# Six scaled pairs in the convolved feed-forward, and fewer resident constants in a two-block kernel

## The chip, the cores and the metric

The kernel runs on one core of a Trainium2 chip. The metric is the device time of one execution in microseconds (us). Before the change it is 1011.3 us, the median of three runs (1009.15 to 1011.61).

Names of the engines: PE is TensorE, which multiplies matrices; DVE is VectorE; ACT is ScalarE; POOL is GpSimd; SP is SyncE, which here only issues transfers. SBUF is the memory that all engines work from, 128 partitions wide; PSUM holds the results of matmuls, in banks of 512 float32 columns.

## The reference, cut to what matters

One sequence of 256 tokens, width 1024, float32, passes two blocks.

```
# first block
hn = rms_norm(h, norm_mix_pre);  p = hn @ w_in            # 6912 columns
p_rw, p_ret, g_rw, g_ret = split(p)
y_rw  = rwkv7_mixer(p_rw, ...)      # 8 heads of 64, state S_t = S diag(w) + rank-one terms, over 256 steps
y_ret = retention_mixer(p_ret, positions)  # 8 heads, rotary q and k (64), v (128), decay masks, silu(g) * norm(o)
merged = sigmoid(g_rw) * (y_rw @ w_branch_rw) + sigmoid(g_ret) * (y_ret @ w_branch_ret)
h = h + rms_norm(merged @ w_out, norm_mix_post)
u = rms_norm(h, norm_ffn_pre) @ ffn_w_up                  # 2 x 2816 columns
u = causal depthwise convolution of width 3 over tokens + bias
gate, val = split(u)
h = h + rms_norm((gelu(gate) * val) @ ffn_w_down, norm_ffn_post)
# second block: SwiGLU, then spatial gating and Mamba-2 side by side, SwiGLU, a gated injection, a final norm
```

The second block isn't touched by the change, but it takes its buffers from the same slab.

## The kernel before, in words

**Weights.** All weights are read once, as a stream of 335 chunks of 128 x 1024 float32 values, eight 128 x 128 tiles each, in the order of use. A chunk is loaded by SP into one of six stage buffers. ACT copies it to float16 (hi) and DVE writes the rest, stage minus hi, as bfloat16 (lo); there are nine hi and lo buffers. A product is three matmuls (hi x hi, hi x lo, lo x hi), so a tile of 128 output columns from 1024 inputs is 24 matmuls of 256 token columns (`mtile`). `token_major` makes products with tokens on the partitions, by matmuls of 512 columns.

**Slab.** Everything that is neither stream, constants nor the residual h lies in one slab of SBUF, SLAB = 32,688 float32 columns. `Slab.get` hands out columns in the order of the program, `Buf.free` gives them back. A buffer that is laid over room used before has to wait until the last user of that room is done. `get` prefers a gap whose last user is planned to end before the new buffer is first needed (hints from the round of planning before), and among these it packs.

**Order of work.** The program is first recorded as a list of operations with their dependences. `Plan.run` is a list planner with a price for each operation and a due time from a run backwards; `Plan.issue` then emits every engine's instructions in the planned order. There are four rounds, each with the slab laid out anew from the times of the one before, and the best plan of the last three is taken. On the chip each engine runs its list in order and waits on semaphores, SP too: a transfer that waits holds up the stage loads behind it.

**First block.** `BlockOne.run` streams w_in: six tiles on the unscaled input, then scaled ones; the value part of retention (RET_V), rotated q and k, the retention gate (RET_G), then 16 tiles of branch gates. Beside these, two generators are stepped by `tick`: `rwkv` and `retention`. They use four "side" PSUM banks, the stream four "main" ones. RET_G fills all four main banks, two at a time; `evac_g` empties each: a tanh on ACT into a new 512-column buffer, then a DVE operation in place. Only after that can the next gate tile have the bank.

`rwkv` prepares four pairs of heads (from w2a2, a selector sel8t, and the RWKV columns), builds the score matrices m4, then solves 32 x 32 triangular systems: lt holds the factors, x starts as a constant (eye32), and 31 steps of two DVE operations each work on x and tmp. x and tmp are written to DRAM (scr_g, scr_h) and read back in other layouts into gb, hb and rb, which POOL has set to zero. Then two chunks of 128 tokens follow one after the other, a norm, and the product with g2.

`retention` works on two quads of heads. For each it multiplies scores by a decay table (3072 columns for both, loaded once) and by the values (2048 columns, both quads together).

**Feed-forward.** `post_norm` ends w_out and also yields xs, the input of the feed-forward without the norm's scaling by row. `up_pairs` makes 22 pairs of a gate and a value tile, each pair in one bank of 512 columns; seven main banks are there in this stage. Pairs 0 to 3 multiply xs, and `evac` scales their results by the norm (a DVE operation of 512 columns out of PSUM), so that PE needn't wait for the norm. Pairs from 4 on multiply `later`, the input scaled by `normed`, and need no scaling. In `evac` follow, for each half of the pair, an ACT operation and two DVE operations of the convolution, then gelu, the product and the split of the result.

Of the kernel before, what the change touches and what calls it, by code (L numbers as in the profile page):

```python
# [45 lines left out]
ZONE = 14000  # L46
ROUNDS = 4
FIRST = 4.0
SLAB = 32688
DECAY_C = float(np.exp(-0.5))  # L50
# [572 lines left out]
class Program:  # L623
# [260 lines left out]
    def up_pairs(self, gname, gbase, uname, ubase, xs, evac, later=None, chunked=False):  # L884


        banks = [self.pair() for _ in range(4)]
        self.mtiles_outer([b[:, 0:T] for b in banks], gname, [("c", gbase + i * P) for i in range(4)], xs, chunked)
        for i in range(NFF):
            if i < 4:  # L890
                bank = banks[i]
            else:
                xs = later or xs
                bank = self.pair()
                self.mtile(bank[:, 0:T], gname, range(NK), ("c", gbase + i * P), xs)
            self.mtile(bank[:, T : 2 * T], uname, range(NK), ("c", ubase + i * P), xs)
            self.done(lambda i=i, bank=bank: evac(i, bank))
        self.flush()
# [97 lines left out]
class BlockOne:  # L996
# [64 lines left out]
    def rwkv(self):  # L1061
        pr = self.pr
        V, S, PE, mm = pr.V, pr.S, pr.PE, pr.PE.matmul
        k_ = pr.k
        w2a2, g2 = pr.col("w2a2", 0, 512), pr.col("g2", 0, 512)
        self.AR, self.B, self.K, self.F = [], [], [], []
# [35 lines left out]
        for t in range(4):  # L1102
# [30 lines left out]
            bank = pr.bank()  # L1133
            mm(bank[:, 0:T], lhsT=k_["sel8t"][:, t * P : t * P + P], rhs=rk.ap, start=True, stop=True)
            kk = pr.buf(T)
# [81 lines left out]
            yield  # L1217
        rk.free()
        self.wdad.free()


        gb, hb, rb = pr.buf(1024), pr.buf(2048), pr.buf(512)
        for b in (gb, rb, hb):
            pr.G.memset(b.ap, 0.0)

# [23 lines left out]
        tv = tmp.v("p (i c) -> p i c", i=32)  # L1249
        V.tensor_copy(x.ap, k_["eye32"])  # L1250
        for j in range(31):
# [5 lines left out]
            if j % 4 == 3:  # L1257
                yield
        V.tensor_copy(tmp.v("p (c i) -> p i c", c=16), xv)
        sg = pr.dram("scr_g", (2, 4, 16, 32, 16))  # L1260
        sh = pr.dram("scr_h", (2, 4, 16, 16, 32))
        pr.plan.sync.dma_start(out=sg.rearrange("a b h i c -> (a b h) (i c)"), in_=x.ap)
        pr.plan.sync.dma_start(out=sh.rearrange("a b h c i -> (a b h) (c i)"), in_=tmp.ap)
        hcs = lambda b: b.v("p (h n) -> p h n", h=16)
        gv, hv, rv = hcs(gb), hcs(hb), hcs(rb)
        for b in range(4):
            s = slice(32 * b, 32 * b + 32)
            for half in range(2):
# [5 lines left out]
                pr.plan.sync.dma_start(out=d, in_=sh[half, b].rearrange("h c i -> c h i"))  # L1274
        for b in (lt, x, tmp):
            b.free()
# [97 lines left out]
        for b in (u, ut, b2, state, hb, m4, r0, vt, bt, kt0, *self.AR, *self.F):  # L1374
            b.free()
        rs = pr.buf(16)
        pr.rsqrt_small(rs.ap, stat.v("p (n k) -> p n k", k=2)[:, :, 1], 16, 1.0, 64e-5)
# [9 lines left out]
        for t in range(4):  # L1387
            bank = pr.bank()
            for c in range(2):
                pr.transpose(bank[:, c * P : c * P + P], ytv[:, c, t * P : t * P + P])  # L1390
            mm(bank[:, T : 2 * T], lhsT=g2[:, t * P : t * P + P], rhs=self.gd.ap, start=True, stop=True)
            o = pr.buf(T)
            S.activation(o.ap, bank[:, 0:T], AF.Identity, scale=pr.col("rw_lnx_w", t), bias=pr.col("rw_lnx_b", t))
            V.tensor_tensor(out=o.ap, in0=o.ap, in1=self.bv[t].ap, op=ADD)
            V.tensor_tensor(out=o.ap, in0=bank[:, T : 2 * T], in1=o.ap, op=MUL)
            self.bv[t].free()
            pr.unbank(bank)
            self.y_rw.append(pr.split(o.ap))
            o.free()
            yield  # L1400
        yt.free()
        self.gd.free()

# [24 lines left out]
    def retention(self):  # L1428
# [3 lines left out]
        for quad in range(2):  # L1432
# [4 lines left out]
            ov = oq[quad].v("p (c n) -> p c n", c=2)  # L1437
            qs, kk = self.rot["q", quad], self.rot["k", quad]
            for pair in range(2):
                banks = [pr.bank(), pr.bank()]  # L1440
# [5 lines left out]
                for i, bank in enumerate(banks):  # L1446
                    h = 4 * quad + 2 * pair + i
                    s = pr.buf(384)
                    V.tensor_tensor(out=s.ap, in0=bank[:, 0 : 3 * P], in1=pr.k["decay"][:, 3 * P * h : 3 * P * h + 3 * P], op=MUL)
                    pr.unbank(bank)  # L1450
                    ss.append(s)
# [3 lines left out]
                for i, s in enumerate(ss):  # L1455
                    h = 4 * quad + 2 * pair + i
                    e = slice(P * i, P * i + P)
                    v0, v1 = self.vr[:, 0, h * P : h * P + P], self.vr[:, 1, h * P : h * P + P]
                    mm(pov[:, 0, e], lhsT=s[:, 0:P], rhs=v0, start=True, stop=True)
                    mm(pov[:, 1, e], lhsT=s[:, P : 2 * P], rhs=v0, start=True, stop=False)  # L1460
                    mm(pov[:, 1, e], lhsT=s[:, 2 * P : 3 * P], rhs=v1, start=False, stop=True)
                    s.free()
                S.activation(ov[:, :, 2 * pair * P : 2 * (pair + 1) * P], pov, AF.Copy)
                pr.unbank(po)
                yield
            for b in qs + kk:
                b.free()
            yield
            for c in range(2):
# [7 lines left out]
                yield  # L1477
        self.vrb.free()
        ov = lambda c, h, n=1: oq[h // 4][:, c * 512 + (h % 4) * P : c * 512 + (h % 4) * P + n * P]
# [33 lines left out]
    def evac_v(self, c, nh, ps):  # L1513
        self.pr.S.activation(self.vr[:, c, 512 * nh : 512 * nh + 512], ps, AF.Copy)

# [14 lines left out]
    def run(self):  # L1530
# [35 lines left out]
        for j, (what, i, c) in enumerate(order):  # L1566
# [11 lines left out]
            if j == 8:  # L1578
                self.angles(pr.ins["pos"])
        dec = pr.buf(3072)  # L1580
        pr.plan.sync.dma_start(out=dec.ap, in_=pr.ins["decay"])
        pr.k["decay"] = dec.ap
        self.vrb = pr.buf(2048)
        self.vr = self.vrb.v("p (c n) -> p c n", c=2)
        pr.token_major("w_in", RET_V, xs, self.evac_v)
# [19 lines left out]
        pr.finish(g_ret)  # L1605
        dec.free()

# [33 lines left out]
        def evac(i, bank):  # L1641
            src, p = bank, None
            if i < 4:
                p = pr.buf(2 * T)
                V.tensor_tensor(out=p.v("p (g n) -> p g n", g=2), in0=bank.rearrange("p (g n) -> p g n", g=2),
                                in1=n2.rb.ap.unsqueeze(1).to_broadcast([P, 2, T]), op=MUL)
                src = p.ap
# [432 lines left out]

_KEEP = ("ones", "ident", "sel2", "sel8t", "inv", "mask", "blk64", "eye32")


def build(tc, ins, out, at, at2):
    nc = tc.nc
    with tc.tile_pool(name="sb", bufs=1) as sb, \
# [6 lines left out]
        hall = sb.tile([P, NK * T], F32, name="h")  # L2093
        cst = sb.tile([P, ins["cst"].shape[1]], F32, name="cst")
        kt = sb.tile([P, sum(ins[n].shape[1] for n in _KEEP)], F32, name="konst")
# [17 lines left out]
def program(pr, hall, kt):  # L2113
# [20 lines left out]
    load("ones", "ident")  # L2134
    load("sel2", "sel8t", "inv")
    pr.plan.sync.dma_start(out=pr.cst[:, nv:], in_=ins["cst"][:, nv:])
    pr.ws.load_to(3)
    load("mask", "blk64", "eye32")
    pr.power = pr.buf(16)
# [35 lines left out]
```

## Time and profile before

| | |
|---|---|
| median of three runs | 1011.3 us (1009.15 to 1011.61) |
| profiled execution | 1015.67 us |
| its span, first to last instruction | 1013.9 us |
| busy: PE, DVE, ACT, POOL | 983.4, 794.5, 613.8, 34.6 us |
| mean granted clock of PE | 0.988 of full speed |
| read from HBM | 185.35 MB, 185 GB/s over the span |

The profile is of one execution. A row of a timeline gives the start and the length of an operation, its engine, the line that issued it (here nearly always L484, the loop in `issue`), what it writes and reads, its form, and in brackets how long the engine stood idle before it and what ended that wait. Matmuls are pipelined, so their lengths overlap; the distance between starts is what one costs. The granted clock has two levels, 2.4 GHz (1.00) and 1.2 GHz (0.5); a stretch in between is a mix.

### The profile page before, as it was taken

What the parts mean: (1) busy time and instruction counts of PE and PEld (TensorE: products, weight loads), DVE (VectorE), ACT (ScalarE), POOL (GpSimd) and SP (SyncE); (2) the same over time, 40 slices, a digit from 0 to 9 for tenths busy, and PEclk for the clock granted to TensorE, in tenths of its full rate; (3) what the DMA queues carried; (4) which work ended last, traced back from release to release, by engine and by line L of the source; (5) the groups of instructions that cost most, each with busy time, mean ns of one, the idle gap of its engine ahead of it and who ended that gap; (6) DMA issues with size and microseconds to landing.
All of it is one profiled execution on the core that took longest, in us unless ns stands there. A gap on an engine that the chain in (4) does not pass through costs nothing.

```text
span 1013.9 us, 22086 instructions
## 1 busy us (share of the span) xinstructions
PE 983.4 (97%) x8884; PEld 830.6 (82%) x8899; DVE 794.5 (78%) x1515; ACT 613.8 (61%) x1042; POOL 34.6 (3%) x35
## 2 busy tenths in 40 slices
PE   8999996999998999999999999999999999999996
PEld 6766745998987888889888888768887888888884
DVE  7999698679888999756977756589798987776654
ACT  6774432545686877556655545577899665554543
POOL 2100000100001000000000000000000000000000
PEclk9899998999999999999999999999999999999999
DMA  9646656246636766664766666655545686666621
GB/s 344 233 150 197 183 166 194 74 155 224 204 96 220 218 203 204 204 197 140 236 204 204 200 198 205 198 179 161 198 124 173 201 273 205 202 196 205 198 75 42
DMA packets 60790, 189.68 MB, mean 187 GB/s; under 512 B 13184, under 2 KB 14992, under 8 KB 60176
## 3 DMA queue, kind: packets, MB, share of 16 engines
q1 hardware_dynamic: 59824, 185.39, 58.6%
q10 hardware_dynamic: 864, 2.89, 0.8%
q8 instruction: 69, 1.13, 0.5%
q14 instruction: 33, 0.27, 0.1%
HBM read 185.35 MB, written 1.85 MB: 185 GB/s over the span
## 4 chain that ended last, share of the span: by engine, by line
PE 71%; DVE 15%; ACT 6%; DMA 4%; issue 3%; POOL 1%; SPq 0%; POOLq 0%; ACTq 0%; DVEq 0%
PE main L484 44%; PE side L484 27%; DVE slab L484 11%; DVE lo L484 4%; ACT slab L484 3%; ACT hi L484 1%; DMA stage<-stream 1%; DMA slab<-scr_cs 1%; PE side L237 1%; DVE h L484 1%; POOL slab L484 1%; ACT L484 1%; DMA slab<-scr_l 1%; DMA h<-xt 1%; DMA scr_cs<-slab 0%
## 5 line engine op out<-in xcount | busy, mean ns | idle before, releaser
L484 PE MATMUL main<-slab,hi 128*128 128x256 f16 (+2 forms) x3276 | 553.7, 270 | 11.9 <-DVE slab L484 10.3
L484 PEld LDWEIGHTS <-hi 128*128 128x128 f16 x5080 | 489.3, 99 | 73.4 <-issue 13.3
L484 ACT ACTIVATE hi<-stage 128x1024 f16<-128x1024 f32 (+1 forms) x338 | 351.8, 1047 | 277.2 <-PE main L484 172.1
L484 DVE TENSOR_TENSOR lo<-stage,hi 128x1024 bf16<-128x1024 f32 (+1 forms) x338 | 406.8, 1210 | 139.3 <-ACT hi L484 138.5
L484 PE MATMUL main<-slab,lo 128*128 128x256 f16 (+1 forms) x1638 | 438.5, 272 | 0.4 <-DVE lo L484 0.4
L484 PE MATMUL side<-slab,hi 128*128 128x256 f16 (+3 forms) x1804 | 278.4, 260 | 2.0 <-DVE slab L484 1.1
L484 PEld LDWEIGHTS <-lo 128*128 128x128 bf16 x2540 | 249.2, 98 | 33.2 <-issue 3.7
L484 PE MATMUL side<-slab,lo 128*128 128x256 f16 (+1 forms) x902 | 225.3, 262 | 0.0
L484 DVE TENSOR_TENSOR slab<-slab 128x256 f32<-128x256 f32 (+13 forms) x427 | 165.5, 405 | 18.0 <-ACT slab L484 15.6
L484 ACT ACTIVATE slab<-slab 128x256 f32<-128x256 f32 (+4 forms) x302 | 116.7, 419 | 34.1 <-DVE slab L484 25.1
L484 PE MATMUL main<-hi,slab 128*128 128x512 f16 (+3 forms) x304 | 83.4, 357 | 0.6
L484 PEld LDWEIGHTS <-slab 128*128 128x128 f16 (+1 forms) x521 | 47.8, 101 | 42.6 <-issue 3.0
L484 ACT ACTIVATE slab<-side 128x128 f32<-128x128 f32 (+5 forms) x93 | 32.1, 379 | 51.8 <-PE side L484 42.5
L484 PEld LDWEIGHTS side<-slab 128*128 128x128 f32 x376 | 51.8, 192 | 8.4 <-DVE slab L484 4.4
L484 PE MATMUL side<-slab 128*128 128x64 f32 (+3 forms) x379 | 56.1, 264 | 2.5 <-DVE slab L484 2.3
L484 POOL TENSOR_TENSOR slab<-slab 128x2 f32<-128x2 f32 (+2 forms) x19 | 28.9, 1518 | 838.5 <-DVE slab L484 825.7
L484 PE MATMUL main<-lo,slab 128*128 128x512 bf16 (+3 forms) x138 | 48.5, 354 | 0.0
L484 DVE TENSOR_TENSOR slab<-side,slab 128x512 f32<-128x512 f32 (+4 forms) x58 | 32.7, 579 | 11.0 <-PE side L484 5.4
L484 DVE SCALAR_TENSOR_TENSOR slab<-main,cst,slab 128x255 f32<-128x255 f32 (+2 forms) x88 | 38.8, 469 | 1.6 <-ACT slab L484 1.5
L484 DVE SCALAR_TENSOR_TENSOR slab<-h,cst,slab 128x256 bf16<-128x256 f32 (+2 forms) x88 | 35.4, 427 | 2.3 <-ACT slab L484 2.2
L484 ACT ACTIVATE slab<-main 128x256 f32<-128x256 f32 (+2 forms) x66 | 25.3, 402 | 15.3 <-DMA scr_g<-slab 6.9
L484 DVE TENSOR_TENSOR slab<-main,slab 128x256 f32<-128x256 f32 (+1 forms) x53 | 28.6, 550 | 5.7 <-PE main L484 4.2
(60 smaller groups left out, 400.9 us busy)
## 6 DMA issues: line engine op xcount, KB each, us to landing
stage<-stream SPq DMA_DIRECT2D x332, 512.0 KB, 4.3
slab<-scr_cs SPq DMA_DIRECT2D x1, 2048.0 KB, 9.3
stage<-stream SPq DMA_DIRECT2D x6, 256.0 KB, 5.5
slab<-decay SPq DMA_DIRECT2D x1, 1536.0 KB, 8.4
slab<-slab SPq DMA_DIRECT2D x32, 32.0 KB, 1.9
slab<-last ACTq DMA_DIRECT2D x1, 1024.0 KB, 7.0
slab<-cst ACTq DMA_DIRECT2D x1, 1024.0 KB, 11.2
h<-xt SPq DMA_DIRECT2D x3, 256.0 KB, 6.1
```

What stands on the lines that cost most here:

```text
L237: op = self.new("PE", lambda: [fn(*args, **kw) for _, fn, args, kw in calls], (), {})
L484: o.fn(*o.args, **o.kw)
```

## The change

- The slab grows by 2048 columns, to 34,736. The room comes from constants that are no longer resident: w2a2 and g2 (1024 columns of cst), sel8t and eye32 (1024 of the constants).
- `rwkv` loads w2a2 and sel8t into slab buffers at its start and frees them after the four pairs of heads. x is loaded from eye32 by a transfer, where DVE copied it. lt is freed after the solve, and gb, hb and rb are taken and zeroed after it, where they were taken before it. g2 is loaded near the end.
- `retention` loads the decay table in two halves, one for each quad, and the values lie in two buffers of 1024; table and values are freed after their quad.
- RAW = 6: pairs 0 to 5 of the convolved feed-forward multiply xs and are scaled at eviction; `later` is used from pair 6 on.

```diff
-SLAB = 32688
+RAW = 6
+SLAB = 34736
@@ up_pairs
         for i in range(NFF):
+            if i >= RAW:
+                xs = later or xs
             if i < 4:
                 bank = banks[i]
             else:
-                xs = later or xs
                 bank = self.pair()
@@ rwkv
-        w2a2, g2 = pr.col("w2a2", 0, 512), pr.col("g2", 0, 512)
+        w2a2b, selb = pr.buf(512), pr.buf(512)
+        a = pr.at["w2a2"][0]
+        pr.plan.sync.dma_start(out=w2a2b.ap, in_=pr.ins["cst"][:, a : a + 512])
+        pr.plan.sync.dma_start(out=selb.ap, in_=pr.ins["sel8t"])
+        w2a2 = w2a2b.ap
...
-            mm(bank[:, 0:T], lhsT=k_["sel8t"][:, t * P : t * P + P], rhs=rk.ap, start=True, stop=True)
+            mm(bank[:, 0:T], lhsT=selb[:, t * P : t * P + P], rhs=rk.ap, start=True, stop=True)
...
-        rk.free()
+        for b in (rk, selb, w2a2b):
+            b.free()
         self.wdad.free()
-        gb, hb, rb = pr.buf(1024), pr.buf(2048), pr.buf(512)
-        for b in (gb, rb, hb):
-            pr.G.memset(b.ap, 0.0)
...
-        V.tensor_copy(x.ap, k_["eye32"])
+        pr.plan.sync.dma_start(out=x.ap, in_=pr.ins["eye32"])
...
         V.tensor_copy(tmp.v("p (c i) -> p i c", c=16), xv)
+        lt.free()
...
         pr.plan.sync.dma_start(out=sh.rearrange("a b h c i -> (a b h) (c i)"), in_=tmp.ap)
+        gb, hb, rb = pr.buf(1024), pr.buf(2048), pr.buf(512)
+        for b in (gb, rb, hb):
+            pr.G.memset(b.ap, 0.0)
...
-        for b in (lt, x, tmp):
+        for b in (x, tmp):
             b.free()
...
+        g2b = pr.buf(512)
+        a = pr.at["g2"][0]
+        pr.plan.sync.dma_start(out=g2b.ap, in_=pr.ins["cst"][:, a : a + 512])
...
-            mm(bank[:, T : 2 * T], lhsT=g2[:, t * P : t * P + P], rhs=self.gd.ap, start=True, stop=True)
+            mm(bank[:, T : 2 * T], lhsT=g2b[:, t * P : t * P + P], rhs=self.gd.ap, start=True, stop=True)
@@ retention
+            dec = pr.buf(1536)
+            pr.plan.sync.dma_start(out=dec.ap, in_=pr.ins["decay"][:, 1536 * quad : 1536 * quad + 1536])
...
-                    V.tensor_tensor(out=s.ap, in0=bank[:, 0 : 3 * P], in1=pr.k["decay"][:, 3 * P * h : 3 * P * h + 3 * P], op=MUL)
+                    d = 3 * P * (h % 4)
+                    V.tensor_tensor(out=s.ap, in0=bank[:, 0 : 3 * P], in1=dec[:, d : d + 3 * P], op=MUL)
...
-            for b in qs + kk:
+            for b in (*qs, *kk, dec, self.vrb[quad]):
                 b.free()
@@ run
-        dec = pr.buf(3072)
-        pr.plan.sync.dma_start(out=dec.ap, in_=pr.ins["decay"])
-        pr.k["decay"] = dec.ap
-        self.vrb = pr.buf(2048)
-        self.vr = self.vrb.v("p (c n) -> p c n", c=2)
+        self.vrb = [pr.buf(1024) for _ in range(2)]
+        self.vr = [b.v("p (c n) -> p c n", c=2) for b in self.vrb]
...
-            if i < 4:
+            if i < RAW:
                 p = pr.buf(2 * T)
@@ build, program
-_KEEP = ("ones", "ident", "sel2", "sel8t", "inv", "mask", "blk64", "eye32")
+_KEEP = ("ones", "ident", "sel2", "inv", "mask", "blk64")
...
-        cst = sb.tile([P, ins["cst"].shape[1]], F32, name="cst")
+        cst = sb.tile([P, at["end"][0]], F32, name="cst")
...
-    load("sel2", "sel8t", "inv")
-    pr.plan.sync.dma_start(out=pr.cst[:, nv:], in_=ins["cst"][:, nv:])
+    load("sel2", "inv")
     pr.ws.load_to(3)
-    load("mask", "blk64", "eye32")
+    load("mask", "blk64")
```

## Rows read from the trace of the kernel before

**Rows 1.** The page's first line and first part: busy us, share of span, instructions.
```profile
span 1013.9 us, 22086 instructions
PE 983.4 (97%) x8884; PEld 830.6 (82%) x8899; DVE 794.5 (78%) x1515; ACT 613.8 (61%) x1042; POOL 34.6 (3%) x35
```

**Rows 2.** Waits of PE: us in total, times, longest.
```profile
PE main L484 <- DVE slab L484: 11.5, 4, 9.0
```

**Rows 3.** Table by stretch: length, busy us (instructions), clock, DMA share, GB/s.
```profile
30.00:40.00 10.00, 9.47 (x62) 7.58 (x61) 8.04 (x19) 7.61 (x15) 2.95 (x1) 0.66 0.59 201
...
176.00:181.00 5.00, 4.94 (x26) 3.49 (x25) 0.60 (x1) 1.44 (x4) 0.00 (x0) 0.53 0.48 64
...
317.00:322.00 5.00, 5.00 (x33) 3.83 (x31) 5.00 (x13) 2.32 (x5) 0.00 (x0) 0.66 0.09 36
330.00:390.00 60.00, 60.00 (x551) 53.09 (x549) 59.90 (x114) 46.36 (x80) 0.00 (x0) 1.00 0.70 210
420.00:460.00 40.00, 40.00 (x405) 35.88 (x403) 19.48 (x21) 18.56 (x28) 0.00 (x0) 1.00 0.67 204
```

**Rows 4.** Chain that ended last, in order of time: start, length, work.
```profile
570.48 21.08 PE main L484 x192
```

**Rows 5.** Timeline of PE, 150 to 176 us.
```profile
150.28 0.38 PE L484 MATMUL main<-lo,slab 128*128 128x512 bf16 x1
...
175.41 0.58 PE L484 MATMUL main<-slab,hi 128*128 128x256 f16 x2 [8.97 <-DVE slab L484]
```

**Rows 6.** Timeline of DVE, 172 to 176 us.
```profile
174.67 0.69 DVE L484 SCALAR_TENSOR_TENSOR slab<-slab,main 128x512 f32<-128x512 f32 x1 [1.49 <-ACT slab L484]
```

**Rows 7.** Timeline of ACT, 167 to 175 us.
```profile
174.04 0.60 ACT L484 ACTIVATE slab<-main 128x512 f32<-128x512 f32 x1 [6.88 <-DMA scr_g<-slab]
```

**Rows 8.** Timeline of SP, 170 to 173 us.
```profile
171.94 0.33 SPq L484 DMA_DIRECT2D scr_g<-slab  x1
```

**Rows 9.** Tile lo, up to 314.5 us: DVE's splits, ns min, median, max.
```profile
L484 DVE TENSOR_TENSOR lo<-stage,hi x94: 683/1215/1226, 4.6 to 312.8; 128x1024 bf16<-128x1024 f32 x88, 128x512 bf16<-128x512 f32 x6
```

**Rows 10.** Timeline of PE, 310 to 317 us.
```profile
311.10 0.71 PE L484 MATMUL side<-konst,slab 128*128 128x128 f32 x4 [1.28 <-POOL slab L484]
...
315.22 0.49 PE L484 MATMUL main<-slab,hi 128*128 128x256 f16 x3 [1.34 <-ACT slab L484]
316.43 0.27 PE L484 MATMUL main<-slab,hi 128*128 128x256 bf16 x1 [0.72 <-DVE slab L484]
```

**Rows 11.** Timeline of POOL, two of the norm's powers.
```profile
307.22 3.82 POOL L484 TENSOR_TENSOR slab<-slab 128x2 f32<-128x2 f32 x1 [15.95 <-DVE slab L484]
...
495.36 0.70 POOL L484 TENSOR_TENSOR slab<-slab 128x2 f32<-128x2 f32 x1 [19.85 <-DVE slab L484]
```

**Rows 12.** Groups by form, DVE, 313.9 to 420 us: count, busy us, mean ns.
```profile
L484 DVE SCALAR_TENSOR_TENSOR slab<-main,cst,slab 128x255 f32<-128x255 f32 x22 | 9.6, 472 | 0.0
...
L484 DVE SCALAR_TENSOR_TENSOR slab<-slab,cst 128x255 f32<-128x255 f32 x8 | 3.6, 476 | 0.0
...
L484 DVE TENSOR_TENSOR slab<-side,slab 128x512 f32<-128x512 f32 x3 | 1.9, 674 | 0.0
```

**Rows 13.** Timelines of SP and of PE near the start.
```profile
12.68 0.33 SPq L484 DMA_DIRECT2D cst<-cst  x1
...
28.92 0.70 PE L237 MATMUL side<-slab,cst 64*128 64x256 f32 x4
```

**Rows 14.** Transfers by line: count, KB each, median us from issue to landing.
```profile
cst<-cst SPq DMA_DIRECT2D x1, 512.0 KB, 6.0
```

**Rows 15.** Groups by form, POOL: count, busy us, mean ns.
```profile
L484 POOL MEMSET slab<- 128x2048 f32 x1 | 1.8, 1810 | 0.0
```

**Rows 16.** Timeline of DVE, 242 to 260 us.
```profile
242.29 0.41 DVE L484 TENSOR_TENSOR slab<-slab 128x256 bf16<-128x256 f32 x1
...
259.00 1.08 DVE L484 SCALAR_TENSOR_TENSOR slab<-slab,main 128x256 f32<-128x256 f32 x3
```

**Rows 17.** Waits of SP's queue: us in total, times, longest.
```profile
SPq L484 <- DVE lo L484: 444.7, 174, 15.8
```

More of the change, by code (lines that the diff above doesn't have):

```diff
@@ L1401, in rwkv @@
         yt.free()
+        g2b.free()
         self.gd.free()
@@ L1457, in retention @@
                     e = slice(P * i, P * i + P)
-                    v0, v1 = self.vr[:, 0, h * P : h * P + P], self.vr[:, 1, h * P : h * P + P]
+                    d = slice(h % 4 * P, h % 4 * P + P)
+                    v0, v1 = self.vr[quad][:, 0, d], self.vr[quad][:, 1, d]
                     mm(pov[:, 0, e], lhsT=s[:, 0:P], rhs=v0, start=True, stop=True)
@@ L1477, in retention @@
                 yield
-        self.vrb.free()
         ov = lambda c, h, n=1: oq[h // 4][:, c * 512 + (h % 4) * P : c * 512 + (h % 4) * P + n * P]
@@ L1513, in evac_v @@
     def evac_v(self, c, nh, ps):
-        self.pr.S.activation(self.vr[:, c, 512 * nh : 512 * nh + 512], ps, AF.Copy)
+        self.pr.S.activation(self.vr[nh][:, c, :], ps, AF.Copy)
     def evac_g(self, c, nh, ps):
@@ L1605, in run @@
         pr.finish(g_ret)
-        dec.free()
         def evac_ret(i, ps):
```

## The prediction

> **What bounds the kernel now.** I read the page's first part, then the waits of TensorE, then tables by stretch, then the timelines around the two long waits. TensorE (PE) is busy 983.4 of 1013.9 us [rows 1], so only time in which it stands or runs at half clock can be had. Of its waits one is large: 11.5 us in four waits on a VectorE (DVE) result, 9.0 of it in one piece [rows 2]. The tables show two places where PE loses time after the start: 166 to 181 us, and 310 to 322 us [rows 3]. Elsewhere between them and after them it issues at full rate: 192 matmuls of 256 columns in 21.08 us, 0.110 us each [rows 4].
>
> The profiled execution took 1015.67 us, 1.8 us more than its span and 4.4 us above the median of the runs, 1011.3. I work out a saving against that execution and take the same number of us off the median.
>
> **Stall A, 166.4 to 175.4 us.** The last 512-column matmul of the retention gate (RET_G) starts at 150.28, yet PE stands 8.97 us until 175.41 for DVE [rows 5]. The DVE operation is the second half of evac_g, at 174.67 [rows 6]. Its first half, the tanh on ScalarE (ACT), started at 174.04, having waited 6.88 us, not for PE but for the transfer scr_g<-slab [rows 7]. That transfer is the one that reads the RWKV solve's x, issued at 171.94 [rows 8]. evac_g has nothing to do with x except room: its 512-column buffer was laid over x, and its twin, which waits for scr_h<-slab in the same way, over tmp. Two main banks therefore stay full some 24 us, and the gate tiles run out of banks. The code's widths say why. With decay table 3072, values 2048, m4 4096, r0, y0 and vt 3072, AR 2048, gb, hb and rb 3584, normed input 2048, rotated q and k 2048, oq 2048, lt, x and tmp 2048, bv 1024, bt and kt0 1024 and some 3000 of small ones, about 31,200 of 32,688 columns are taken when the last two evac_g ask for 1024.
>
> Afterwards PE is cold: in 176 to 181 its granted clock is 0.53 [rows 3], between the levels 1.2 and 2.4 GHz, after it had stood 9 us. That costs 5.0 x (1 - 0.53) = 2.35 us. Stall A costs 8.97 + 2.35 = 11.3 us.
>
> The change takes, at that moment, 1536 columns from the table (one quad at a time) and 3584 from gb, hb and rb (now taken after the solve), and adds 2048 to the slab: some 26,100 of 34,736 taken, 8600 free. w2a2b and selb are gone by then (freed with rk). I count on room whose last user is long done, so the whole 11.3 us. What is late next: PE goes on with gate tiles. Up to 314 us, 94 pieces are split, of which six are halves, so 91 chunks [rows 9]; PE has used 664 weight tiles by then (w_in 432, w_branch_ret 64, w_branch_rw 32, w_out 64, two fills 8, four gate and four value tiles 64), 83 chunks of eight. Eight chunks of 24 matmuls at 0.110 us are 21 us of weights ahead, so weights are not the next wait.
>
> **Stall B, 310 to 322 us.** PE stands three times: 1.28 us before 311.10, for the GpSimd (POOL) power of the norm, and 1.34 and 0.72 us before 315.22 and 316.43, for the normed input `later` [rows 10]. Then 317 to 322 runs at clock 0.66 [rows 3]: 5.0 x 0.34 = 1.7 us. With RAW 6, pairs 4 and 5 use the unscaled xs, which are there: 2 x 48 matmuls at 0.110 us are 10.5 us of cover, while PE waited only 2.1 us for `later`. So 1.34 + 0.72 + 1.7 = 3.8 us go. The 1.28 us stay or go with where the planner puts the spread matmul; bounds 0 and 1.28, I take 0.6, the middle, since either is one decision of the planner.
>
> This wait has a cause of its own: the power took 3.82 us at 307.22 and 0.70 us at 495.36 [rows 11]. The Trainium skill ("SBUF — State Buffer", section "SBUF: two separate sides") has a rule for it: a GpSimd operation that reads SBUF and a VectorE operation with two SBUF inputs lock each other out for whole instructions. This trace agrees, 3.82 us beside weight splits against 0.70 us. By that rule the power stays slow, as the splits stay, and the sum would be 0.6 us less.
>
> The two more scalings cost DVE 2 x 0.674 = 1.35 us [rows 12]. The convolution's operations on a scaled pair read SBUF instead of PSUM, 0.476 against 0.472 us each. DVE is full there, 59.9 of 60 us from 330 to 390, but 19.5 of 40 from 420 to 460 [rows 3]. What hides the cost is this slack: PE is not waiting for DVE in that stage, and the last product of the 22 is wanted only at the end of the 4 x 22 x 3 matmuls of the down projection's first four outputs, 29 us. Without this cover it would be 1.35 us plus the 5 us by which PE now runs ahead.
>
> **The other parts.** Removed: one copy of eye32 on DVE, 512 columns, at most the 0.674 us of a 512-column operation out of PSUM [rows 12] and at a time when PE waits for nothing, so 0 (bounds 0 and 0.7 gained). Transfers: the whole volume stays. At the start, 1 MB of constants and half of the decay table drop out, and 0.5 MB (w2a2b and selb) come in. The constants' tail with w2a2 was issued at 12.68, took 6.0 us, and its first reader ran at 28.92 [rows 13, 14]: 10 us of slack. Bounds for the new order: at best the start gains 0.7 us of small waits, at worst w2a2b is issued behind the stage loads and costs 3 us. I take 0, because SyncE's (SP's) list reaches it early whenever its room is fresh. The second half of the table, eye32 and g2b are issued later on SP, each with a possible wait for room in front of stage loads; 0 as long as the wait is below the weights' lead. The memsets of gb, hb and rb, 3584 columns at 1.81 us for 2048 [rows 15], 3.2 us on POOL, move behind the solve; 0 if they run during the round trip of the solve's result, 3.2 at worst, on the RWKV chain only.
>
> Everything is planned anew, so small waits will move about. I set 1.0 us against the gain for this, an estimate from the waits of 0.7 to 1.3 us in stall B [rows 10], bounds -2 and +4.
>
> Sum: 11.3 + 3.8 + 0.6 - 1.0 = 14.7 us. Profiled 1001.0, median 1011.3 - 14.7 = 996.6, said as 997.
>
> **The rivals.**
> 1. *The RWKV tail takes A's place.* The last part of y_rw is split at 242.29; the first four outputs of w_branch_rw are evacuated at 259.00, so their 48 matmuls (5.3 us) start near 253.7 [rows 16]. These 11 us of slack are what A's removal eats. If the solve and the chain behind it don't move, each us of delay stands on PE: the memsets' 3.2 us and about 2 us of half clock, 1002. Against: the chain shares PE with gate tiles that now run before 181, and DVE has idle time behind the solve.
> 2. *B stays in another form*, for DVE is full there and `later` must still be made: only A counts, 1011.3 - 11.3 = 1000.
> 3. *The slab trick does nothing*: the allocator again puts evac_g over x, or the next PSUM bank is late for another reason. B alone, 1007. Against: 8600 free columns.
> 4. *Better*: the start moves as well. From 30 to 40 us the clock is 0.66 [rows 3], 3.4 us lost. If PE's order there changes so that it stays warm, 994.
> 5. *Slower*: a transfer into reused room (second half table, eye32, g2b) stands at the head of SP's queue, with the stage loads behind it in order. PE starves once the hold exceeds the weights ahead, 21 us by the count above. SP stood up to 15.8 us in one wait before, with no harm that shows [rows 17]. A hold of 40 us would cost 19 us and 2 us of half clock: 1011.3 - 14.7 + 21 = 1018. It makes the kernel slower from a hold of some 36 us (21 and 14.7), so the plan would have to be wrong by that much; stall A, the worst seen, is 9.
>
> **How the numbers follow.** Forecast 0.50 (993 to 1000), rival 1 0.15, rival 2 0.15, rival 3 0.05, rival 4 0.09, rival 5 0.06. The range holds the forecast, rivals 1, 2 and 4 and the bounds of replanning: 991 to 1005. A change below 0.3%, 3 us, can't be told from none. Faster: all but rival 5 and half of rival 3's spread, and a little for a new wait that I don't see: 0.90; same 0.04; slower 0.06.
>
> **What would show it.** Right: no wait over 2 us on PE between 150 and 200 us; ACT's tanh of RET_G follows its matmuls within a few us, released by PE; PE's table has clock 1.00 from 150 to 300; pair 4 of the feed-forward starts with no wait for `later`, and six scalings of 512 columns stand in place of four. Wrong: PE waits on the solve's transfers again, on the splits of y_rw before w_branch_rw, on weights (ACT or DVE behind stage<-stream), or a late w2a2b near 29 us.

## The result, and the profile after

The changed kernel takes 999.8 us (median of 4 runs, 995.1 to 1001.3) against 1010.2 for the kernel before on the same chip (4 runs, 1009.0 to 1011.6): ratio 0.989 [0.985, 0.992], 10.4 us less. A second measurement beside the first experiments gave 12.2 us less (ratio 0.987, below). 997 with a range of 991 to 1005 was forecast. The profiled execution took 1000.74 us, 14.9 less than that of before, where 14.7 were worked out.

The page, its first line and first part [rows 1]: the engines have the same work to do, PE is busy 7.8 us less, and its idle time fell from 30.5 to 23.2 us.

```profile
span 998.8 us, 22101 instructions
...
PE 975.6 (98%) x8899; PEld 829.1 (83%) x8899; DVE 794.5 (80%) x1516; ACT 609.7 (61%) x1038; POOL 29.8 (3%) x35
```

The waits of PE (us in total, times, longest). The 9.0 us wait for DVE [rows 2] is gone; what is left are many small ones.

```profile
PE side L485 <- DVE slab L485: 4.5, 6, 2.2
PE side L485 <- ACT slab L485: 4.1, 3, 2.0
...
PE side L485 <- DMA slab<-scr_g: 0.8, 1, 0.8
```

**Where stall A was.** ACT's timeline of the changed kernel from 148 us: the last two tanhs of RET_G follow their matmuls at once, the first released by PE, where one came at 174.04 after 6.88 us of waiting for the solve's transfer [rows 7].

```profile
148.71 0.60 ACT L485 ACTIVATE slab<-main 128x512 f32<-128x512 f32 x1 [1.10 <-PE main L485]
...
150.15 0.59 ACT L485 ACTIVATE slab<-main 128x512 f32<-128x512 f32 x1
```

DVE's timeline: evac_g's second half, 174.67 before [rows 6], is done by 152.5.

```profile
151.78 0.68 DVE L485 SCALAR_TENSOR_TENSOR slab<-slab,main 128x512 f32<-128x512 f32 x1
```

The table by stretch (length, then busy us and instructions of PE, PEld, DVE, ACT, POOL, then the granted clock, DMA share, GB/s). The first two answer to 166 to 181 us, the last three to 305 to 322 us [rows 3, 10]: PE full, clock 1.00.

```profile
166.00:176.00 10.00, 10.00 (x94) 8.90 (x93) 7.76 (x17) 4.86 (x9) 0.00 (x0) 1.00 0.86 266
176.00:181.00 5.00, 5.00 (x47) 4.25 (x44) 2.45 (x2) 2.40 (x5) 0.00 (x0) 1.00 0.85 208
...
305.00:312.00 7.00, 7.00 (x67) 6.26 (x65) 7.00 (x19) 5.89 (x13) 0.00 (x0) 1.00 0.29 85
312.00:317.00 5.00, 5.00 (x48) 4.45 (x46) 5.00 (x6) 4.87 (x9) 0.00 (x0) 1.00 0.46 131
317.00:322.00 5.00, 5.00 (x48) 4.45 (x47) 5.00 (x10) 4.97 (x8) 0.00 (x0) 1.00 0.97 342
```

**Where stall B was.** No wait of PE for the scaled input is left, six scalings of 512 columns (0.68 us each) stand where four stood, and the power before it took 0.70 us instead of 3.82 [rows 11]. POOL's timeline of the changed kernel:

```profile
273.47 1.41 POOL L485 TENSOR_TENSOR slab<-slab 128x1 f32<-128x1 f32 x1 [43.07 <-ACT slab L485]
...
299.78 0.70 POOL L485 TENSOR_TENSOR slab<-slab 128x2 f32<-128x2 f32 x1 [19.82 <-DVE slab L485]
450.81 1.52 POOL L485 TENSOR_TENSOR slab<-slab 128x1 f32<-128x1 f32 x1 [150.32 <-DVE slab L485]
```

**The whole span in four stretches.** Three events stand in both kernels: RET_G's last 512-column matmul (150.28 before, 148.94 after), the norm's power that ends the first block's mixer (284.26, 273.47), and the same of the feed-forward (467.97, 450.81). The table by stretch between them, first the kernel before:

```profile
0.00:150.28 150.28, 144.67 (x986) 101.27 (x995) 129.52 (x279) 89.16 (x158) 10.55 (x17) 0.98 0.66 211
150.28:284.26 133.98, 123.94 (x1217) 112.79 (x1216) 102.89 (x255) 65.41 (x116) 7.60 (x4) 0.96 0.53 169
284.26:467.97 183.71, 179.34 (x1818) 159.42 (x1817) 152.53 (x287) 122.03 (x214) 6.29 (x3) 0.99 0.61 188
467.97:1013.90 545.93, 535.42 (x4872) 457.18 (x4875) 409.60 (x697) 337.25 (x555) 10.20 (x12) 1.00 0.59 185
```

and the changed kernel:

```profile
0.00:148.94 148.94, 140.59 (x995) 98.99 (x996) 131.45 (x279) 89.29 (x158) 10.30 (x18) 0.99 0.67 219
148.94:273.47 124.53, 122.25 (x1218) 112.15 (x1217) 99.52 (x255) 64.93 (x117) 5.80 (x2) 1.00 0.53 167
273.47:450.81 177.34, 176.79 (x1815) 159.10 (x1813) 152.59 (x289) 123.06 (x214) 2.90 (x4) 1.00 0.64 200
450.81:998.80 547.99, 535.97 (x4881) 458.84 (x4878) 410.89 (x697) 332.41 (x552) 10.78 (x12) 0.99 0.58 184
```

Length less PE's busy time is its idle time. By that:

| stretch | length | PE idle | PE busy |
|---|---|---|---|
| start to RET_G | -1.34 | +2.74 | -4.08 |
| rest of the mixer (stall A) | -9.45 | -7.76 | -1.69 |
| feed-forward (stall B) | -6.37 | -3.82 | -2.55 |
| from there to the end | +2.06 | +1.51 | +0.55 |
| sum | -15.1 | -7.3 | -7.8 |

The same two stretches can be read in the traces of all experiments below. The mixer's takes 123.6 to 129.5 us in the seven traces of kernels that take both the table and the values per quad, and 131.4 to 141.5 us in the five others (the kernel before: 133.98). The feed-forward's takes 177.3 to 177.9 us in the six traces with six or eight pairs, and 180.9 to 184.5 us in the six with four.

### The profile page after: what moved, and what is told of

It is laid out like the page before. It is cut to its first block, busy times and chain, and to the rows that moved or that the text cites. A ratio compares the mean times of both kernels' runs of the same rounds, so it can differ in the third digit from the quotient of the medians.

```text
span 998.8 us, 22101 instructions
## 1 busy us (share of the span) xinstructions
PE 975.6 (98%) x8899; PEld 829.1 (83%) x8899; DVE 794.5 (80%) x1516; ACT 609.7 (61%) x1038; POOL 29.8 (3%) x35
## 4 chain that ended last, share of the span: by engine, by line
PE 83%; DVE 7%; DMA 5%; ACT 3%; issue 2%; SPq 1%; POOLq 0%; POOL 0%; ACTq 0%; DVEq 0%
PE main L485 52%; PE side L485 30%; DVE slab L485 5%; ACT slab L485 2%; DVE lo L485 2%; PE side L238 1%; DMA slab<-scr_cs 1%; DMA stage<-stream 1%; DVE h L485 1%; DMA slab<-cst 1%; ACT hi L485 1%; DMA h<-xt 1%; SPq L485 1%; DMA scr_h<-slab 1%; DMA slab<-scr_l 0%
## 5 line engine op out<-in xcount | busy, mean ns | idle before, releaser
L485 ACT ACTIVATE slab<-slab 128x256 f32<-128x256 f32 (+3 forms) x302 | 117.1, 419 | 35.5 <-DVE slab L485 28.1
L485 PE MATMUL side<-slab 128*128 128x64 f32 (+3 forms) x396 | 60.6, 270 | 3.7 <-DVE slab L485 2.8
L485 PEld LDWEIGHTS side<-slab 128*128 128x128 f32 x392 | 54.3, 192 | 9.5 <-DVE slab L485 4.9
L485 PE MATMUL main<-lo,slab 128*128 128x512 bf16 (+3 forms) x152 | 53.8, 356 | 0.0
L485 POOL TENSOR_TENSOR slab<-slab 128x2 f32<-128x2 f32 (+2 forms) x19 | 24.1, 1267 | 963.9 <-DVE slab L485 920.8
L485 DVE TENSOR_TENSOR slab<-main,slab 128x512 f32<-128x512 f32 (+1 forms) x55 | 29.9, 556 | 7.6 <-PE main L485 5.4
L485 DVE SCALAR_TENSOR_TENSOR slab<-main,cst,slab 128x255 f32<-128x255 f32 (+2 forms) x80 | 34.8, 468 | 1.0 <-ACT slab L485 0.9
L485 ACT ACTIVATE slab<-h,cst 128x256 f16<-128x256 f32 (+1 forms) x64 | 27.1, 443 | 6.9 <-DVE h L485 3.9
```

What stands on the lines that cost most here:

```text
L485: o.fn(*o.args, **o.kw)
```

## The experiments

Ten runs were made, in three groups, each with the kernel before on the same chip (medians 1010.6, 1010.9 and 1009.8 us; all its runs lay between 1006.8 and 1013.9). "Against before" is the difference of medians.

| kernel | time, us | against before | ratio, interval |
|---|---|---|---|
| changed kernel again | 998.4 | -12.2 | 0.987 [0.985, 0.989] |
| six pairs only | 1012.9 | +2.3 | 1.002 [1.001, 1.004] |
| slab part only | 1002.7 | -7.9 | 0.992 [0.990, 0.994] |
| retention quads only | 1002.2 | -8.4 | 0.992 [0.989, 0.994] |
| changed, no growth | 997.5 | -13.3 | 0.987 [0.986, 0.989] |
| gb, hb, rb late only | 1021.0 | +10.1 | 1.011 [1.009, 1.012] |
| quads and six pairs | 999.4 | -11.4 | 0.989 [0.987, 0.991] |
| changed, eight pairs | 999.5 | -11.4 | 0.989 [0.987, 0.991] |
| decay table per quad only | 1008.8 | -1.0 | 0.999 [0.998, 1.000] |
| values per quad only | 1006.6 | -3.2 | 0.996 [0.994, 0.997] |

**1. The changed kernel again**, unedited, to have it beside the rest.

> The changed kernel once more, timed in more rounds, since the two profiled executions differ by 15 us and the medians only by 10. Theory 1 (the two long waits and the half clock behind them are the gain): 10 to 15 us below before, ratio 0.985 to 0.990; PE has no wait over 2.5 us between 10 and 900 us. Rival 2 (the gain is luck of a new plan and of one execution): the ratio falls back towards 0.995.

Measured 998.4 (995.5 to 999.9), no wait over 1.8 us, so theory 1. But the half clock isn't wholly gone: in this second trace of the same program PE waits 1.79 us for the solve's read-back, where it waited 0.75 us in the first, and behind it the clock is 0.50 for three microseconds. PE's timeline and the table:

```profile
181.62 0.43 PE L485 MATMUL side<-slab 128*128 128x64 f32 x2 [1.79 <-DMA slab<-scr_g]
```

```profile
182.00:185.00 3.00, 3.00 (x19) 3.00 (x18) 0.00 (x0) 1.70 (x5) 0.00 (x0) 0.50 0.47 81
```

**2. Six pairs only**: the kernel before with the feed-forward's part of the change.

```
+RAW = 6
-                xs = later or xs            # at i >= 4
+            if i >= RAW:
+                xs = later or xs
-            if i < 4:                        # in evac
+            if i < RAW:
```

> The kernel before with RAW = 6 alone. Theory 1: the wait for `later` (1.34 and 0.72 us) and the half clock behind it go, the slab wait of 9 us before a gate tile stays: 3.8 to 5.0 us below before, ratio 0.995 to 0.996. Rival 2 (replanning): anything within 2 us of before. Rival 3 (DVE, full in that stage, takes the gain back): within 1 us of before, and PE waits on DVE later in the 22 pairs.

Measured 1012.9, slower, which none of the three had. At its own place the part did what it was made for: from the mixer's power (286.11) to the feed-forward's (464.00) are 177.9 us, 5.8 less than in the kernel before, with no wait for `later`. But the mixer got longer. PE's timeline, the slab's stall in another form, and the table from 166 us:

```profile
173.73 5.78 PE L485 MATMUL side<-slab 128*128 128x64 f32 x26 [11.06 <-DMA slab<-scr_g]
```

```profile
166.00:176.00 10.00, 2.27 (x11) 2.30 (x11) 0.50 (x1) 1.44 (x4) 0.05 (x1) 0.50 0.46 96
176.00:186.00 10.00, 10.00 (x49) 9.49 (x49) 1.02 (x2) 1.14 (x3) 0.52 (x1) 0.50 0.00 0
```

PE stood 11.1 us instead of 9.0 and then ran at the lower level until 186. Nothing of the edit is there; it is the new plan, in whose layout the last two of evac_g's buffers lie on x and on rb, which is read later still.

**3. The slab part only**: the changed kernel with four pairs.

```
-RAW = 6
+RAW = 4
```

> The changed kernel with RAW = 4, so the slab part alone. Theory 1: the slab wait of 9 us and its half clock are gone, the waits for `later` are back: 9 to 11 us below before, ratio 0.989 to 0.991; together with the feed-forward part alone it adds up to the whole within 2 us. Rival 2: the parts don't add up.

Measured 1002.7. Stall A is gone, stall B is back; PE's timeline:

```profile
303.45 0.49 PE L485 MATMUL main<-slab,hi 128*128 128x256 f16 x3 [1.76 <-ACT slab L485]
304.93 0.37 PE L485 MATMUL main<-slab,hi 128*128 128x256 bf16 x1 [0.98 <-DVE slab L485]
```

The gain of 7.9 us is less than the 9 to 11 expected, and the parts alone add up to -7.9 + 2.3 = -5.6 us, not to the whole's -12.2: rival 2. On top of this part the six pairs are worth 12.2 - 7.9 = 4.3 us.

**4. Retention quads only**: the kernel before with nothing but the decay table and the values taken per quad.

```
+            dec = pr.buf(1536)               # per quad; its half of the table loaded into it
-            for b in qs + kk:
+            for b in (*qs, *kk, dec, self.vrb[quad]):
-        dec = pr.buf(3072)
-        self.vrb = pr.buf(2048)
+        self.vrb = [pr.buf(1024) for _ in range(2)]
```

> The kernel before with only the retention part: decay table and values in two halves, each freed after its quad; slab, constants, solve and RAW as before. In the plan of the changed kernel the gate's evacuation buffers lie in the values and the table of quad 0. Theory 1a (these frees are what ends the slab wait): the 9 us wait is gone or below 2 us, 8 to 11 us below before. Rival 1b (it takes the 2048 added columns or the late gb, hb and rb): the wait stays at 5 us or more, less than 4 us below before.

Measured 1002.2: the whole gain of the slab part (-8.4 against -7.9), as theory 1a had it. PE's timeline shows three short waits in the place of the long one, the longest above the 2 us of theory 1a:

```profile
171.18 0.38 PE L484 MATMUL main<-slab,hi 128*128 128x256 f16 x2 [1.57 <-DVE slab L484]
...
175.67 0.38 PE L484 MATMUL main<-slab,hi 128*128 128x256 f16 x2 [1.70 <-ACT slab L484]
...
182.20 0.41 PE L484 MATMUL side<-slab 128*128 128x64 f32 x2 [2.98 <-DMA slab<-scr_h]
```

The first two are stall A in small. With the quads only, one of evac_g's buffers still lies on room of the solve (lt), so its tanh waits for the solve's last step on DVE, and the next evacuation waits for the transfer out of x. ACT's timeline:

```profile
169.81 0.60 ACT L484 ACTIVATE slab<-main 128x512 f32<-128x512 f32 x1 [1.56 <-DVE slab L484]
175.23 0.38 ACT L484 ACTIVATE slab<-main 128x256 f32<-128x256 f32 x1 [4.83 <-DMA scr_g<-slab]
```

The table by stretch shows the clock at 1.00 all the same:

```profile
166.00:176.00 10.00, 6.73 (x62) 5.68 (x60) 4.82 (x14) 2.70 (x5) 0.00 (x0) 1.00 0.72 234
176.00:181.00 5.00, 3.22 (x30) 2.60 (x27) 1.22 (x1) 1.21 (x4) 0.00 (x0) 1.00 0.43 49
```

**5. No growth**: the changed kernel in the old width.

```
-SLAB = 34736
+SLAB = 32688
```

> The changed kernel with the slab's width back at 32688 columns. Theory (the retention quads alone give the room, the growth is spare): no wait over 3 us on PE between 150 and 200 us, time within 3 us of the changed kernel's 998.4, so 995 to 1002. Rival (my room account, in which 2048 of the 8600 free columns are the growth, is tight): a wait of 5 us or more comes back at 166 to 186 us and the time is 1003 to 1010.

Measured 997.5, as fast as the changed kernel. The 2048 columns aren't needed. The largest wait, and the clock behind it:

```profile
180.44 4.12 PE L485 MATMUL side<-slab 128*128 128x64 f32 x28 [2.53 <-DMA slab<-scr_g]
```

```profile
181.00:196.00 15.00, 15.00 (x101) 14.36 (x101) 6.49 (x21) 5.88 (x14) 0.67 (x1) 0.66 0.59 199
```

**6. gb, hb and rb late**, nothing else.

```
-        gb, hb, rb = pr.buf(1024), pr.buf(2048), pr.buf(512)   # before the solve
+        lt.free()                                              # after the solve
+        gb, hb, rb = pr.buf(1024), pr.buf(2048), pr.buf(512)
```

> The kernel before, with only gb, hb and rb (3584 columns) taken after the solve and lt freed before them. My prediction's account gives these columns 3584 of the 5120 freed, so by it the 9 us wait at 166 us goes and the time is 1000 to 1004. Theory after the trace of the changed kernel (the memsets still run at 0.7 us in it, so nothing is freed by this edit): a wait of 5 to 12 us on the solve's transfer stays between 160 and 190 us, time 1007 to 1014.

Measured 1021.0: slower than both theories allow. My prediction's account is refuted by it. My second theory had the stall right and its reason wrong: unlike in the changed kernel, memsets do move here, those of rb and hb (512 and 2048 columns) to 94.93 and 98.25, since the two are now laid over used room. The last two of evac_g's buffers lie on tmp and on rb in this layout. PE's and ACT's timelines show the price, the last tanhs of RET_G 13 and 17 us after the last one of the kernel before (174.04 [rows 7]):

```profile
174.25 5.78 PE L484 MATMUL side<-slab 128*128 128x64 f32 x26 [7.32 <-DMA slab<-scr_h]
```

```profile
187.56 0.59 ACT L484 ACTIVATE slab<-main 128x512 f32<-128x512 f32 x1
...
191.51 0.60 ACT L484 ACTIVATE slab<-main 128x512 f32<-128x512 f32 x1 [0.95 <-PE side L484]
```

```profile
176.00:200.00 24.00, 23.07 (x134) 21.80 (x135) 11.62 (x40) 5.10 (x11) 3.41 (x2) 0.61 0.00 1
```

24 us at clock 0.61 are 9.0 us lost (23.07 x 0.39), more than the wait itself.

**7. Quads and six pairs**, the two edits of experiments 4 and 2 together and nothing else of the change.

```
+RAW = 6
+            dec = pr.buf(1536)               # and so on, as in 2 and 4
```

> The kernel before with two edits only: decay table and values taken per quad, and six unscaled pairs. Theory (the growth of 2.3 us with six unscaled pairs alone is the slab stall made longer by a new plan; without that stall the pairs give what they gave on top of the slab part, 4.3 us): 1002.2 - 4.3 = 998, range 995 to 1001, no wait over 3 us between 150 and 200 us, none for the scaled input at 300 to 312 us. Rival (six pairs are worth nothing by themselves, and the 4.3 us come from a lucky plan of the whole changed kernel): 1001 to 1005.

Measured 999.4, no wait over 1.8 us. The loss of experiment 2 was the slab's, for the feed-forward takes the same time in both (177.4 and 177.9 us): with the room given, six pairs bring 11.4 - 8.4 = 3.0 us more, where alone they cost 2.3. These two edits give what the whole change gives.

**8. Eight pairs** in the changed kernel.

```
-RAW = 6
+RAW = 8
```

> The changed kernel with eight instead of six unscaled pairs. Theory (six pairs already cover the wait for the scaled input; DVE is full from 315 to 375 us and gets 1.35 us more): within 2 us of the changed kernel, 997 to 1002, no new wait over 1.5 us for DVE at 300 to 375 us. Rival (the cover of 10.5 us is too short or the wait of the norm is longer, so more pairs gain again): 993 to 996. Second rival (DVE's extra scalings come late and PE waits for the products): 1002 to 1006.

Measured 999.5, the same as six; PE has no wait over 0.2 us between 290 and 375 us in either, and the added scalings don't show.

**9 and 10. One half of the quads' edit each**: only the decay table per quad, or only the values.

```
+            dec = pr.buf(1536)               # 9: per quad, freed after it
-        dec = pr.buf(3072)
...
+        self.vrb = [pr.buf(1024) for _ in range(2)]   # 10: the first freed after quad 0
-        self.vrb = pr.buf(2048)
```

> The kernel before with only the decay table taken per quad (1536 columns each, the first half freed after quad 0); the values stay one buffer. The gate's last two results want 1024 columns. Theory (any 1024 columns whose last reader is quad 0 are enough): the table's half does it alone, no wait over 3.5 us on PE between 150 and 200 us, 1000 to 1004. Rival (both halves, 2560 columns, are needed, since other buffers take the first ones that come free): a wait of 5 us or more on the solve's transfer, 1007 to 1014.

> The kernel before with only the values taken per quad (1024 columns each, the first half freed after quad 0); the decay table stays one buffer. Theory (any 1024 columns whose last reader is quad 0 are enough): 1024 columns are just what the gate's last two results want, so no wait over 3.5 us on PE between 150 and 200 us, 1000 to 1004. Rival (just enough is not enough, since another buffer takes a part of it first): a wait of 5 us or more on the solve's transfer, 1007 to 1014.

Measured 1008.8 and 1006.6: my theory (any 1024 columns do) is wrong in both, the sum of the two halves (-4.2) is half of what both give. With the values only, one tanh still waits for scr_g, that is, for the room of x, and the last, laid over gb, comes only at 186.07. ACT's and PE's timelines:

```profile
170.47 0.60 ACT L484 ACTIVATE slab<-main 128x512 f32<-128x512 f32 x1 [5.54 <-DMA scr_g<-slab]
```

```profile
171.84 0.58 PE L484 MATMUL main<-slab,hi 128*128 128x256 f16 x2 [6.89 <-DVE slab L484]
```

With the table only, evac_g has room (its last operation starts at 153.30), and PE has main tiles until 174.4. But then it waits for the solve's read-back, goes on with a row of RWKV matmuls at the lower level, and stands 4.3 of 12 us from 300 us on:

```profile
178.41 5.73 PE L484 MATMUL side<-slab 128*128 128x64 f32 x26 [4.05 <-DMA slab<-scr_h]
```

```profile
176.00:192.00 16.00, 13.60 (x67) 13.11 (x67) 2.37 (x5) 4.27 (x12) 0.00 (x0) 0.58 0.37 102
...
300.00:312.00 12.00, 7.72 (x66) 6.36 (x64) 8.71 (x15) 5.66 (x10) 3.82 (x1) 0.98 0.89 326
```

So neither rival came true as it stood. The table alone met the rival's time, but with evac_g's room given and a wait of 4.05 us, below its 5; the values alone showed its mechanism, with a time between the two ranges. That some other buffer lacked room with the table only is not shown.

## Why the prediction was right, and where it wasn't

**Bound and stalls: right.** The two places read from the table were the ones that moved: -9.45 and -6.37 of -15.1 us lie there. That 14.7 us were worked out and 14.9 profiled is luck in part: stall A gave 1.9 us less than its term, stall B 2.0 us more.

**Stall A's cause: right; its remedy's account: wrong.** evac_g's buffers wanted room whose last user was the solve; give other room, and the tanhs run at 148.71 and 150.15. But the step "takes 1536 columns from the table and 3584 from gb, hb and rb, and adds 2048: 8600 free" failed. The growth is spare (experiment 5). gb, hb and rb late free nothing: the program records the solve ahead of the last two of evac_g's buffers, so the three are taken by then in either order.

The allocator of each kernel gives the count. When those two buffers are asked for, 28,018 columns are taken in the kernel before (the sum of widths had some 31,200), 28,018 with gb, hb and rb late, and 25,458 in the changed kernel as in that with the quads only. The difference is 2560, the table's half of 1536 and the values' half of 1024, and the values' half wasn't in my sum of freed room at all. That 34,736 - 25,458 = 9278 free columns lie near my 8600 is luck.

In the kernel before and in the changed one alike, gb, hb and rb lie in room never used and are zeroed among the first memsets; alone, the edit costs 10.1 us (experiment 6). POOL's timelines, before and changed (the one memset more is of ob, a buffer used after the solve, zeroed at 171.77 before):

```profile
0.73 4.74 POOL L484 MEMSET slab<- 128x16 f32 x11 [0.29 <-POOLq L2157]
```

```profile
0.72 5.63 POOL L485 MEMSET slab<- 128x16 f32 x12 [0.29 <-POOLq L2168]
```

In the program, the last two of evac_g's buffers lay on the columns of x and tmp before; after, three of the four lie on quad 0's values and decay table, the fourth in a small old room. Before, 32,688 - 28,018 = 4670 columns were free when the last two asked. Of the pieces wide enough for 512, all but one had a last user planned at 161 us or later, and that one was passed over: `get` goes by the time of need in the round of planning before, 174.5 and 176.7 us, so x and tmp, planned to be free by 163, counted as in time. In the changed kernel that time is 143.8 and 145.2. A delay of one round thus stands as the need of the next; what this alone is worth was not tested. A count of free columns says nothing on who used them last, and that is what the wait hangs on.

**Stall A's size: mis-sized, 9.45 in place of 11.3, and 6.73 in the second trace of the changed kernel.** The wait of 8.97 went whole. Waits of 0.75 (the solve's read-back, 181.81), 1.16 (216.03) and 0.20 us came in its place, and PE's busy time fell by 1.69, where 2.35 were put down to the clock. In medians, experiments 3 and 4 give 7.9 and 8.4, but not all of that is stall A: with the quads only, the mixer's stretch is 5.2 us shorter than before, and the rest lies in stretches that this kernel doesn't edit.

**Stall B: right in kind, mis-sized the other way, 6.37 in place of 4.4.** The waits for `later` and the half clock behind them are gone (0.72 + 1.34 and 1.7), and the power's wait, for which 0.6 was taken between 0 and 1.28, went whole. That leaves 6.37 - 3.82 - 1.7 = 0.85 us of busy time that I can't place. In medians the part is worth 3.0 (experiment 7) to 4.3 us (experiment 3). Of all stretches this one repeats best: 177.34 us in both traces of the changed kernel. That its extra scalings are hidden holds even for eight pairs.

**The page's rule on the power.** Weighed in the prediction was the Trainium skill's "SBUF — State Buffer", section "SBUF: two separate sides": a GpSimd operation that reads SBUF and a VectorE operation with two SBUF inputs lock each other out for whole instructions. What it says of the lock, the traces bear out. DVE of the kernel with the quads only splits without a break from 299.76, for 3.51 us, and POOL's power, begun at 300.01, ends 0.56 us after:

```profile
299.76 3.51 DVE L484 TENSOR_TENSOR lo<-stage,hi 128x1024 bf16<-128x1024 f32 x3
```

```profile
300.01 3.82 POOL L484 TENSOR_TENSOR slab<-slab 128x2 f32<-128x2 f32 x1 [15.95 <-DVE slab L484]
```

With gb, hb and rb late it is four splits, 4.63 us from 309.79, and a power of 5.02 us that also ends 0.56 us behind them. What I drew from it, that the power stays slow because the splits stay, was wrong: in the changed kernel DVE has a gap there, and the power fits into it. DVE's timeline:

```profile
299.49 0.15 DVE L485 TENSOR_SCALAR slab<-side 128x2 f32<-128x2 f32 x1
300.38 1.23 DVE L485 TENSOR_TENSOR lo<-stage,hi 128x1024 bf16<-128x1024 f32 x1 [0.74 <-ACT hi L485]
```

All six traces with six or eight pairs have 0.70 us there; those with four have 2.68 to 5.02. Presumably the plan is in less of a hurry for the norm and orders the splits otherwise; which of its decisions makes the gap was not isolated.

**The other parts.** The start was put at 0 (bounds -0.7 and +3) and gained 1.34 us in the trace: 2.74 us more waits (1.79 at 7.33, 1.58 at 27.87), 4.08 less busy time. As the kernel with quads and six pairs does without any of the start's edits and is as fast (999.4 against 998.4), they are worth about nothing. The replanning, put at -1.0 us (bounds -2, +4), is the start and the last row of the table: +1.34 - 2.06 = -0.7. In the second trace of the same program these two gain 2.57 and 1.03 us, so one trace doesn't size this term.

**From one execution to the medians.** The forecast took the profiled saving off the median. 15.1 us of span became 10.4 and 12.2 us of median, because the profiled execution of before (1015.67) was 5.4 us above the median of its runs and that of after (1000.74) 0.9 above. A part of what I summed was that execution's own. Some of it goes with the clock: over the 17 runs of the kernel before beside the first experiments, the mean granted clock lies between 0.987 and 0.995, and a line through them falls by 0.7 us for each 0.001. The profiled execution had 0.988, their median 0.992, so by this estimate some 2.7 us of its excess are clock. Which stretches vary can be seen in the changed kernel, which has two traces. The table by stretch of the second (experiment 1), cut at the same events:

```profile
0.00:147.71 147.71, 141.67 (x987) 100.30 (x995) 131.59 (x279) 89.33 (x158) 10.30 (x18) 0.98 0.67 220
147.71:274.96 127.25, 123.83 (x1218) 113.79 (x1217) 99.52 (x255) 64.97 (x117) 5.79 (x2) 0.99 0.53 164
274.96:452.30 177.34, 176.73 (x1814) 159.10 (x1813) 152.62 (x289) 123.02 (x214) 2.90 (x3) 1.00 0.63 200
452.30:997.20 544.90, 534.28 (x4875) 457.86 (x4878) 411.05 (x697) 331.95 (x552) 10.78 (x12) 0.99 0.59 185
```

Between two executions of one program the mixer's stretch differs by 2.7 us (the wait of 1.79 us and the half clock behind it), the last one, where nothing was edited, by 3.1 us, and the feed-forward's not at all. In those two stretches, gains of 2 or 3 us can't be read from one trace of each kernel.

**The rivals.** None came. Rival 1 was closest: the solve's read-back is what PE waits for next (0.75 to 2.98 us at 180 to 183 in the kernels with both halves per quad), but w_branch_rw didn't wait. Of rival 4's clock a part came: 30 to 40 us has 0.83 in the changed kernel's first trace, where it had 0.66 [rows 3], but 0.74 in its second, and no 994. Rival 5 was wrong on the hold, though its sign did turn up: two kernels with one part each were slower, by new plans, not by SP's queue. Of these I had thought only as "small waits move about".

**A faster version** than the changed kernel was not found. Without the growth it is equal (997.5), and two of its edits alone are within its run-to-run spread (999.4).

## What to carry to other kernels

When an operation waits for a transfer that has nothing to do with it, look whose room its result is laid over; then free earlier what has the earliest last reader. How much is enough must be measured: half the room gave 1 and 3 us where the whole gave 8.4, and with the table's half alone the operation had its room and PE waited at another place. In a kernel that is planned as a whole, parts don't add: one part cost 2.3 us alone and brought 3.0 to 4.3 beside the other, so measure them in combination before dropping one. Before taking a saving off the median, see how far the profiled execution lies from it.

## What the runs showed of the hardware

What a wait costs afterwards in clock isn't in proportion to it. Behind 8.97 us the table has 0.53 for 5 us [rows 3], and behind 6.89 us 0.50 for 5 us (experiment 10), with tiles of the stream as PE's next work in both. Behind 11.06 us it has 0.50 for 10 us (experiment 2), behind 7.32 us 0.61 for 24 us (experiment 6), behind 4.05 us 0.58 for 16 us (with a part of the standing in it, experiment 9), and behind 2.53 us 0.66 for 15 us (experiment 5). In these four PE's next work was 26 to 28 RWKV matmuls of 64 float32 columns in one row, with no tile of the stream between them.

Through three waits of 1.57, 1.70 and 2.98 us the clock stayed at 1.00 (experiment 4). There the same matmuls follow the wait of 2.98 us by twos, with a stream matmul of 256 columns after every two. But that mixture isn't enough to keep the clock: in experiment 1 the same matmuls by twos follow a wait of 1.79 us, and the clock fell to 0.50 from 182 to 185. So the price of a wait, 0 to 9 us here, can't be read from its length, and not from the work behind it alone. What decides it isn't shown.
